# A two-layer encoder trunk on one core: the order of a few weight splits, a norm's tiles, and where one layer's modulation sums stand

## The chip, the cores and the metric

The kernel runs on one core of a Trainium2 chip. The metric is the device time of one launch in microseconds (us): 2183.36 is the median of three runs of the kernel before. PE (TensorE) does the matrix products, ACT (ScalarE) and DVE (VectorE) the work on rows, POOL (GpSimd) a few small copies, SP (SyncE) starts the transfers. A matrix product writes into PSUM, which has eight banks here.

## What is computed

One sequence of 256 tokens with 2048 features passes two layers. Every layer has an attention part and an MLP, each behind a root-mean-square norm that is modulated by a vector `c`:

```python
for l in range(DEPTH):                                  # 2 layers
    mod = cond @ w_ada[l] + b_ada[l]                    # cond = silu(c); 2048 -> 6 * 2048
    sh_a, sc_a, g_a, sh_m, sc_m, g_m = split(mod, 6)
    h = rmsnorm(x) * (1.0 + sc_a) + sh_a
    proj = h @ w_in[l]
    out_a = diff_attention(...)                         # half of the heads
    q = rmsnorm(cq, q_norm_g[l]) @ w_uq[l]              # latent attention: the other half
    kv = rmsnorm(ckv, kv_norm_g[l]) @ w_ukv[l]          # k_nope and the values v_m
    out_b = mla_attention(...)
    x = x + g_a * (concat(out_a, out_b) @ w_o[l])
    h = rmsnorm(x) * (1.0 + sc_m) + sh_m
    y = square(relu(h @ w_mlp_in[l])) @ w_mlp_out[l]    # 2048 -> 8192 -> 2048
    x = x + g_m * y
return rmsnorm(x, final_norm_g)
```

## The kernel before

The residual `x` stays on the chip with features along the partitions: 16 blocks of 128 features by 256 tokens. All weights come from memory as float32, mostly in 1 MB tiles.

**Split weights.** `weights` (L142) loads a tile `raw` through SP's queue, ACT copies each half of it into a rounded `hi` (L151), and DVE subtracts to get the rest, `lo` (L154). Activations are split in the same way. A product is then three matmuls: hi by hi, hi by lo, lo by hi (`mac`, L192 to L194). There are four buffers for `hi`, four for `lo` and five for `raw`. `wides` (L203) does the MLP's first product for two weight tiles in a bank each.

**Modulation.** A row block of `w_ada` is one more 1 MB tile, `ada`, in the same five `raw` buffers. `ada_load` (L297) starts its transfer, `ada_sums` (L303) reduces it on DVE in one instruction (L310). `weights` counts a `rate` for each tile that it loads: each time that the count reaches one, one modulation tile is loaded and later summed. Each stretch of the program has its own rate. `most` limits how many loaded tiles are summed.

**Order.** Outside the blocks under `manual_schedule`, a scheduler orders the instructions of an engine by the dependences; `follow(a, b)` is an added dependence, without a wait on the chip if both are on one engine. Inside those blocks PE's order is that of the code.

**The four places of the change.**
- *Layer 0, latent values.* `up_v` (L795) loads `w_uv`. Its two `hi` copies follow `self.copied`, the last `copy` (L282) that the code had made: here the copy `aT` of a transposed attention matrix. The products with `w_uv` are L263 to L265.
- *Layer 0, end of the attention part.* The output product adds into `x` in pairs of feature blocks (`update`, L1119). For the last pair, `pair` (L219) puts both products in the two halves of one bank.
- *Layer 0, norm ahead of the MLP.* `rstd` (L554): ACT squares the last pair of blocks one by one (`sqa`, L542); PE sums every square over the features with a constant matrix of which one column is used (`sums`, L569); ACT takes the root of two columns (L577), DVE the reciprocal (L578); PE spreads the result over the partitions by transposes (L584), ACT copies that out of PSUM (`rstd`, L588). Then `modulated` (L655) makes the input `h` of the MLP two blocks at a time: `ht` on DVE (L663), `hi` on ACT (L666), `lo` on DVE (L667). `norm_then_by_k` (L696) feeds them into six banks `pk`, 12 of the MLP's 64 hidden blocks, with two 768-column weight tiles for each pair of blocks. The squared ReLU of these six banks (`relu2`, L1136: Relu L1139, Square L1143, split L185 and L186) comes in `mlp` (L938) behind the first pair of `wides`, whose own halves are joined by `joined` (L1125).
- *Layer 1, norm ahead of the MLP.* `ahead_rest` (L628) works on the sums of the norm beside products `pa` that don't need them yet, at a modulation rate of 0.6 (`RATE_K`). The argument `loads` keeps the rate as it was found until that step of the loop; here it is left at 0.

Of the kernel before, what the change touches and what calls it, by code (L numbers as in the profile page):

```python
# [105 lines left out]
class Trunk:  # L106
# [35 lines left out]
    def weights(self, src, width=2048, after=None):  # L142
# [4 lines left out]
        for i in range(2):  # L147
# [3 lines left out]
            ins = nc.scalar.activation(hi, v, AF.Copy)  # L151
            if after is not None:
                self.follow(ins, after)
            ins = nc.vector.tensor_tensor(lo, v, hi.bitcast(F32), ALU.subtract)  # L154
            if self.hold is not None:
                self.follow(ins, self.hold)
# [46 lines left out]
    def wides(self, srcs, xs):  # L203
# [5 lines left out]
        ws = [self.weights(src, nk * P) for src in srcs]  # L209
# [9 lines left out]
    def pair(self, srcs, xs):  # L219
        ps = self.bank("ps")  # L220
        for j, src in enumerate(srcs):
            self.tile_cols(ps[:, j], src, xs)
        return ps

# [4 lines left out]
    def by_k(self, banks, srcs, xs, k0, nk, n=4, whole=None):  # L229
# [3 lines left out]
        for b, src in enumerate(srcs):  # L233
# [5 lines left out]
            else:  # L239
                w = self.weights(src, width)  # L240
# [295 lines left out]
    def sumsq(self, acc, val, alone=False, scale=1.0):  # L536

        nc = self.nc
        if alone:
            for i in range(2):  # L540
                t = self.tp.tile([P, T], F32, tag="t", name=self.name("sqa"))
                nc.scalar.activation(t, val[:, i], AF.Square)  # L542
# [11 lines left out]
    def rstd(self, acc, n):  # L554

        return self.spread(*self.total(acc, n))
# [9 lines left out]
    def sums(self, ps, a, n, first, last):  # L566

        for t in range(2):
            self.nc.tensor.matmul(  # L569
                ps[:, 0, t : t + 1], a[:, t * P : (t + 1) * P], self.mean[n][:, :1],  # L570
# [3 lines left out]
    def root(self, ps):  # L574
        nc = self.nc
        r = self.s("root")
        nc.scalar.activation(r, ps[:, 0, :2], AF.Sqrt, bias=self.eps)  # L577
        nc.vector.reciprocal(r, r)  # L578
        return ps, r
# [116 lines left out]
    def norm_then_by_k(self, l, acc, sh, sc, src, n, nwhole, fill=(), early=()):  # L696


        r = self.rstd(acc, D) if l or sh else acc
        banks = self.open_banks(2 * n)  # L700
        h = []
        for p in range(8):
# [9 lines left out]
            h += self.modulated(r, k, self.mod[l, sh], self.mod[l, sc], whole, self.lo if p - 1 in early else None)  # L712
# [8 lines left out]
            for b in range(2):  # L721
                self.by_k(banks[b * n :], [src[l, p, b]], h, k, NK, 2 * n, whole)
# [13 lines left out]
    def layer(self, l, acc, st):  # L736
# [173 lines left out]
        with self.tc.manual_schedule(engines={mybir.EngineType.PE}) if l else nullcontext():  # L910
            for m in range(4, NK, 2):
# [3 lines left out]
                if l == 0 and m == NK - 2:  # L915
                    self.update(m, self.pair(srcs, o), g)
# [21 lines left out]
    def mlp(self, l, h, first, g):  # L938
# [4 lines left out]
        nxt = None if l == DEPTH - 1 else self.ahead(l + 1, 0, 1, io["w_a1"][0])  # L943
        for fb in range(NFB):
# [446 lines left out]
```

## Time and profile before

| | |
|---|---|
| three runs, us | 2185.09, 2180.95, 2183.36 |
| median, us | 2183.36 |
| profiled execution, us | 2182.21 |
| its span, us | 2180.4 |
| granted clock of PE, mean over the span | 0.998 of full speed |

The profile shows one execution, taken by the hardware. Its times are us from the start of the span. A row of the timeline holds the start, the duration of a run of like instructions, the engine and line, the output and input by the program's names, the count, and in brackets the idle time of the engine just before with the instruction that ended it. PE's instructions overlap, so their durations add up to more than the time between their starts. A row of the windows holds the stretch and its length, then for PE, PEld (weight loads), DVE, ACT and POOL the busy time and the count, then the granted clock (1.00 is full speed), the busy share of the transfer engines and GB/s.

### The profile page before, as it was taken

The page shows a single profiled execution, that of the slowest core. Times are in us where ns is not written, and L with a number is a line of the kernel's source. Part 1 is how long each engine was busy: PE and PEld are TensorE (multiplying, and loading weights), DVE is VectorE, ACT ScalarE, POOL GpSimd, SP SyncE. Part 2 cuts the span into 40 slices and gives each one's busy share as a digit, 9 for nine tenths or more (in the row PEclk, how much of TensorE's full clock was granted, in tenths as well). Part 3 has the DMA queues.
Part 4 walks back from the last instruction along what each step waited for, and adds up shares of the span by engine and source line. Part 5 has one row for each costly group of instructions (what it writes and reads, how often), then busy time and mean ns, then how long its engine had stood idle before and what let it go on. Part 6 is the DMA issues. An engine that isn't in the chain of part 4 may idle for free.

```text
span 2180.4 us, 30393 instructions
## 1 busy us (share of the span) xinstructions
PE 2157.0 (99%) x12016; PEld 1888.5 (87%) x12016; DVE 1606.6 (74%) x2160; ACT 1153.0 (53%) x1739; POOL 23.3 (1%) x43
## 2 busy tenths in 40 slices
PE   8999999999999999999999999999999999999998
PEld 7899898988888888888898888999888888888886
DVE  8999888887778778778798876798544545555566
ACT  6565664454455355355456565547446535534544
POOL 0000000000000000000001000000000000000000
PEclk9999999999999999999999999999999999999999
DMA  9987888799879888888777666686555555555552
GB/s 400 424 331 275 333 314 310 270 345 344 326 301 343 331 302 341 309 312 330 287 251 270 253 239 226 247 303 240 193 193 193 193 193 188 187 195 189 189 196 95
DMA packets 85538, 586.41 MB, mean 269 GB/s; under 512 B 9489, under 2 KB 9489, under 8 KB 19345
## 3 DMA queue, kind: packets, MB, share of 16 engines
q1 hardware_dynamic: 85106, 583.84, 72.7%
q8 instruction: 94, 1.54, 0.3%
q10 hardware_dynamic: 288, 0.62, 0.1%
q14 instruction: 50, 0.41, 0.1%
HBM read 582.33 MB, written 2.10 MB: 268 GB/s over the span
## 4 chain that ended last, share of the span: by engine, by line
PE 94%; DVE 3%; DMA 2%; ACT 1%; issue 0%; DVEq 0%; ACTq 0%
PE ps L213 25%; PE ps L216 13%; PE py L1092 11%; PE py L1090 11%; PE py L1094 11%; PE pk L249 3%; PE pk L194 2%; PE pk L193 2%; PE pk L192 2%; PE pv L263 1%; PE pv L264 1%; PE pv L265 1%; DVE ada L310 1%; PE pa L194 1%; PE pa L192 1%; PE pa L193 1%
## 5 line engine op out<-in xcount | busy, mean ns | idle before, releaser
L154 DVE TENSOR_TENSOR lo<-raw,hi 128x1024 fp32r<-128x1024 f32 (+1 forms) x720 | 849.8, 1196 | 475.0 <-ACT hi L151 305.9
L151 ACT ACTIVATE hi<-raw 128x1024 fp32r<-128x1024 f32 (+1 forms) x720 | 736.9, 1035 | 649.9 <-PE py L1094 361.5
L213 PE MATMUL ps<-h,hi 128*128 128x512 f32 x2016 | 471.0, 391 | 0.9 <-ACT hi L151 0.9
L213 PEld LDWEIGHTS ps<-h,hi 128*128 128x128 f32 x2016 | 375.0, 188 | 76.9 <-ACT hi L151 1.3
L310 DVE SCALAR_TENSOR_TENSOR ada<-ada,cond 128x2048 f32<-128x2048 f32 x191 | 435.4, 2286 | 2.8 <-ACT sqx L389 2.0
L1090 PE MATMUL py<-hi,hid 128*128 128x512 f32 x1024 | 326.6, 390 | 0.0
L1092 PE MATMUL py<-lo,hid 128*128 128x512 f32 x1024 | 326.1, 389 | 0.0
L1094 PE MATMUL py<-hi,hid 128*128 128x512 f32 x1024 | 325.9, 389 | 0.0
L216 PEld LDWEIGHTS ps<-h,lo 128*128 128x128 f32 x2016 | 250.2, 192 | 4.9
L216 PE MATMUL ps<-h,lo 128*128 128x256 f32 x2016 | 251.7, 283 | 0.0
L1092 PEld LDWEIGHTS py<-lo,hid 128*128 128x128 f32 x1024 | 192.3, 188 | 40.3 <-DVE lo L154 0.4
L1094 PEld LDWEIGHTS py<-hi,hid 128*128 128x128 f32 x1024 | 192.3, 188 | 40.0
L1090 PEld LDWEIGHTS py<-hi,hid 128*128 128x128 f32 x1024 | 191.3, 188 | 38.7
L1129 ACT ACTIVATE sum<-ps 128x256 f32<-128x256 f32 x110 | 42.1, 383 | 128.2 <-PE ps L216 127.9
L192 PE MATMUL pk<-h,hi 128*128 128x256 f32 x304 | 86.0, 289 | 2.3 <-ACT h L666 1.5
L194 PE MATMUL pk<-h,lo 128*128 128x256 f32 x304 | 85.7, 286 | 1.0 <-DVE lo L154 1.0
L193 PE MATMUL pk<-h,hi 128*128 128x256 f32 x304 | 86.1, 285 | 0.1
L186 DVE TENSOR_TENSOR hid<-relu,hid 128x256 fp32r<-128x256 f32 x128 | 48.3, 422 | 45.8 <-ACT hid L185 45.8
L249 PE MATMUL pk<-hf,w 128*128 128x256 f32 x288 | 63.2, 380 | 0.0
L249 PEld LDWEIGHTS pk<-hf,w 128*128 128x128 f32 x288 | 54.5, 190 | 7.8 <-ACT hf L671 0.5
L192 PEld LDWEIGHTS pk<-h,hi 128*128 128x128 f32 x304 | 58.5, 195 | 3.0 <-ACT h L666 1.8
L1139 ACT ACTIVATE relu<-sum 128x512 f32<-128x512 f32 x55 | 34.6, 630 | 48.0 <-DVE sum L1131 47.9
(271 smaller groups left out, 2583.5 us busy)
## 6 DMA issues: line engine op xcount, KB each, us to landing
raw<-in_w_m SPq DMA_DIRECT2D x238, 1024.0 KB, 4.9
ada<-in_w_ada SPq DMA_DIRECT2D x191, 1024.0 KB, 5.0
raw<-in_w_ob SPq DMA_DIRECT2D x24, 1024.0 KB, 4.9
raw<-in_w_dv SPq DMA_DIRECT2D x16, 1024.0 KB, 4.9
raw<-in_w_q SPq DMA_DIRECT2D x16, 1024.0 KB, 4.8
raw<-in_w_n SPq DMA_DIRECT2D x16, 768.0 KB, 5.9
w<-in_w_a SPq DMA_DIRECT2D x24, 384.0 KB, 13.1
raw<-in_w_a SPq DMA_DIRECT2D x12, 768.0 KB, 5.8
```

The source lines that it names most:

```text
L151: ins = nc.scalar.activation(hi, v, AF.Copy)
L154: ins = nc.vector.tensor_tensor(lo, v, hi.bitcast(F32), ALU.subtract)
L192: mm(ps, hi, x[0], start=first, stop=False, skip_group_check=shared)
L193: mm(ps, hi, x[1], start=False, stop=False, skip_group_check=shared)
L194: mm(ps, lo, x[0], start=False, stop=last, skip_group_check=shared)
L213: mm(ps.rearrange("p a b -> p (a b)"), part(w, 0, k), both, start=k == 0, stop=False)
L216: mm(ps[:, 0], part(w, 1, k), x, start=False, stop=k == nk - 1)
L249: self.nc.tensor.matmul(ps, w[i][:, j * P : j * P + P], whole[i], start=first, stop=last, skip_group_check=True)
L310: ins = nc.vector.scalar_tensor_tensor(w, w, 1.0, self.cond, ALU.mult, ALU.mult, accum_out=acc[:, i : i + 1])
L1090: mm(o, xh[:, tok], hi[:, part[j]], start=start, stop=False)
L1092: mm(o, xh[:, tok], lo[:, part[j]], start=False, stop=False)
L1094: mm(o, xl[:, tok], hi[:, part[j]], start=False, stop=stop)
```

## The change

- `up_v` in layer 0: the `hi` copies of `w_uv` follow `spun`, the last `qr` copy of `up_r`, instead of the `aT` copy. On ACT the order of these five goes from `qr, qr, aT, hi, hi` to `qr, qr, hi, hi, aT`.
- The last pair of the output product in layer 0: two banks, each added into `x` as it is done; `pair` is gone.
- `sums` uses all 128 columns of the constant, so that every one of 128 columns holds the sum; `root` reads one column of each half. `rstd` also returns the spread in PSUM, and the first `modulated` of the norm reads it there (`near`). The copy L588 is still made for the others.
- In that norm's first step, the second weight tile's second `hi` follows the last `sqa`, and its second `lo` follows the reciprocal.
- The first Relu of the six banks follows the norm's last `hi`, the next ones the `hi` copies of the first `wides`.
- Layer 0's first `wides` in the MLP: its `joined` and `relu2` come after the second `wides` (`held`).
- Layer 1's norm: rate 0 until step 5 of `ahead_rest`.

The diff, with unchanged lines and the removal of `pair` cut:

```diff
     def weights(self, src, width=2048, after=None, first=0):
...
-            ins = nc.scalar.activation(hi, v, AF.Copy)
-            if after is not None:
+            ins = self.high = nc.scalar.activation(hi, v, AF.Copy)
+            if after is not None and i >= first:
                 self.follow(ins, after)
             ins = nc.vector.tensor_tensor(lo, v, hi.bitcast(F32), ALU.subtract)
-            if self.hold is not None:
+            if self.hold is not None and i >= first:
                 self.follow(ins, self.hold)
...
     # wides
+        ws, self.highs = [], []
+        for src in srcs:
+            ws.append(self.weights(src, nk * P))
+            self.highs.append(self.high)
...
     # by_k
-                w = self.weights(src, width)
+                w = self.weights(src, width, after, int(after is not None))
...
     def rstd(self, acc, n):
-        return self.spread(*self.total(acc, n))
+        ps, r = self.total(acc, n)
+        return self.spread(ps, r), ps[:, 1]
...
     # sums
-                ps[:, 0, t : t + 1], a[:, t * P : (t + 1) * P], self.mean[n][:, :1],
+                ps[:, 0, t * P : (t + 1) * P], a[:, t * P : (t + 1) * P], self.mean[n],
...
     # norm_then_by_k
-        r = self.rstd(acc, D) if l or sh else acc
+        r, near = self.rstd(acc, D) if sh else (acc, acc)
...
+            of = r if p else near
+            h += self.modulated(of, k, self.mod[l, sh], self.mod[l, sc], whole, self.lo if p - 1 in early else None)
...
             for b in range(2):
-                self.by_k(banks[b * n :], [src[l, p, b]], h, k, NK, 2 * n, whole)
+                later = self.squared if sh and p == 0 and b else None
+                if later:
+                    self.hold = self.inverse
+                self.by_k(banks[b * n :], [src[l, p, b]], h, k, NK, 2 * n, whole, later)
...
         def up_r():
             raw = [self.copy(ps, "qr", ms) for ps in self.small(io["w_uq"][l, 2], cq, 4)]
+            self.spun = self.copied
...
         def up_v():
-            w = self.weights(io["w_uv"][l], after=None if l else self.copied)
+            w = self.weights(io["w_uv"][l], after=None if l else self.spun)
...
                 if l == 0 and m == NK - 2:
-                    self.update(m, self.pair(srcs, o), g)
+                    pss = [self.bank("ps")[:, 0] for _ in srcs]
+                    for ps, src in zip(pss, srcs):
+                        self.tile_cols(ps, src, o)
+                    self.update(m, pss, g)
...
-            self.rate = RATE_K
+            self.rate = 0.0 if st else RATE_K
             if st:
-                h = self.ahead_rest(st, 0, acc, 2)
+                h = self.ahead_rest(st, 0, acc, 2, 5)
...
-                first = NNORM, lambda: [self.relu2(b) for b in banks]
-                first = NNORM, lambda: [self.relu2(b) for b in banks]
+                high = self.high
+                first = NNORM, lambda: [
+                    self.relu2(b, after=a) for b, a in zip(banks, [high, *self.highs, *self.highs[1:] * 3])
+                ]
...
     # mlp
-                hid += self.relu2(self.joined(pss, self.t("sum")))
+                    if l == 0:
+                        held = [pss]
+                        continue
+                for ps in held + [pss]:
+                    hid += self.relu2(self.joined(ps, self.t("sum")))
+                held = []
...
     # relu2
-            self.nc.scalar.activation(r, ps, AF.Relu)
+            ins = self.nc.scalar.activation(r, ps, AF.Relu)
+            if after is not None:
+                self.follow(ins, after)
```

What the change does to the engines' orders is shown at three places. The rows are in program order; numbers behind a name tell buffers of one name apart, and `x2` stands for two like instructions in a row. First DVE before, at the norm ahead of layer 0's MLP (`lo` L154 of the first weight tiles, `x` the last update, `root` the reciprocal, `ht` the first modulated blocks):

```order
L154 TENSOR_TENSOR lo_3892<-raw_3889,hi_3891 128x768
L154 TENSOR_TENSOR lo_3896<-raw_3889,hi_3895 128x768
L154 TENSOR_TENSOR lo_3938<-raw_3935,hi_3937 128x768
L1123 SCALAR_TENSOR_TENSOR x<-ps_3730,mod_83,x 128x256 x2
L154 TENSOR_TENSOR lo_3942<-raw_3935,hi_3941 128x768
L578 RECIPROCAL root_3867<-root_3867 128x2
L663 SCALAR_TENSOR_TENSOR ht_3880<-x,mod_87,rstd_3872 128x256 x2
```

and DVE there after the change:

```order
L1138 SCALAR_TENSOR_TENSOR x<-ps_3730,mod_83,x 128x256
L154 TENSOR_TENSOR lo_3893<-raw_3890,hi_3892 128x768
L154 TENSOR_TENSOR lo_3897<-raw_3890,hi_3896 128x768
L154 TENSOR_TENSOR lo_3939<-raw_3936,hi_3938 128x768
L1138 SCALAR_TENSOR_TENSOR x<-ps_3731,mod_83,x 128x256
L576 RECIPROCAL root_3868<-root_3868 128x2
L154 TENSOR_TENSOR lo_3943<-raw_3936,hi_3942 128x768
L661 SCALAR_TENSOR_TENSOR ht_3881<-x,mod_87,pn_3859 128x256 x2
```

The first of the two `x` updates has moved ahead of three `lo`, the fourth `lo` from before the reciprocal to behind it, and `ht` reads `pn`, the spread in PSUM.

Second, ACT at the end of that norm, before (`pk` are the six banks, `hi` of 768 columns the norm's last weight tile, `hi` of 1024 columns the first tile of the first `wides`; the second tile's two `hi` come eleven rows further on):

```order
L1139 ACTIVATE relu_4820<-pk_3874 128x512
L1143 ACTIVATE relu_4820<-relu_4820 128x512
L151 ACTIVATE hi_4681<-raw_4679 128x768
L151 ACTIVATE hi_4685<-raw_4679 128x768
L185 ACTIVATE hid_4823<-relu_4820 128x256
L185 ACTIVATE hid_4824<-relu_4820 128x256
L1139 ACTIVATE relu_4829<-pk_3875 128x512
L1139 ACTIVATE relu_4838<-pk_3876 128x512
L151 ACTIVATE hi_4732<-raw_4730 128x1024
L151 ACTIVATE hi_4736<-raw_4730 128x1024
```

and after the change:

```order
L151 ACTIVATE hi_4682<-raw_4680 128x768
L151 ACTIVATE hi_4686<-raw_4680 128x768
L1154 ACTIVATE relu_4821<-pk_3875 128x512
L1160 ACTIVATE relu_4821<-relu_4821 128x512
L185 ACTIVATE hid_4824<-relu_4821 128x256
L185 ACTIVATE hid_4825<-relu_4821 128x256
L151 ACTIVATE hi_4733<-raw_4731 128x1024
L151 ACTIVATE hi_4737<-raw_4731 128x1024
L1154 ACTIVATE relu_4830<-pk_3876 128x512
L1160 ACTIVATE relu_4830<-relu_4830 128x512
```

Each pair of `hi` now stands ahead of the Relu and Square that were in front of it; the second tile's two `hi` follow two rows further on.

Third, DVE in layer 1's norm, before (`ada` the modulation sum, `al` the low part of the products' input, `lo` the weights of `pa`):

```order
L154 TENSOR_TENSOR lo_13528<-raw_13525,hi_13527 128x768
L154 TENSOR_TENSOR lo_13532<-raw_13525,hi_13531 128x768
L310 SCALAR_TENSOR_TENSOR ada_13471,macc_102<-ada_13471,cond 128x2048
L614 SCALAR_TENSOR_TENSOR al_13510<-x,mod_99,ah_13509 128x256 x2
L578 RECIPROCAL root_13522<-root_13522 128x2
L154 TENSOR_TENSOR lo_13596<-raw_13593,hi_13595 128x768
```

and after the change:

```order
L154 TENSOR_TENSOR lo_13527<-raw_13524,hi_13526 128x768
L154 TENSOR_TENSOR lo_13531<-raw_13524,hi_13530 128x768
L154 TENSOR_TENSOR lo_13594<-raw_13591,hi_13593 128x768
L612 SCALAR_TENSOR_TENSOR al_13509<-x,mod_99,ah_13508 128x256 x2
L154 TENSOR_TENSOR lo_13598<-raw_13591,hi_13597 128x768
L576 RECIPROCAL root_13521<-root_13521 128x2
```

The sum between the weight splits is gone. It and a second one of the same norm, which stood just ahead of `lo_13726`, come some 30 rows later, in the MLP, and their two loads move back by six places on SP.

More of the change, by code (lines that the diff above doesn't have):

```diff
@@ L139, in bank, with weights @@
         return self.pp.tile([P, 2, T], F32, tag="b", name=self.name(name))
-    def weights(self, src, width=2048, after=None):
+    def weights(self, src, width=2048, after=None, first=0):
         nc = self.nc
@@ L217, in wides, with by_k @@
         return pss
[L219 to L223, printed above, removed]
     def open_banks(self, n):
         return [self.bank("pk") for _ in range(n)]
-    def by_k(self, banks, srcs, xs, k0, nk, n=4, whole=None):
+    def by_k(self, banks, srcs, xs, k0, nk, n=4, whole=None, after=None):
         kpb = srcs[0].shape[-1] // (n * P)
```

11 lines of the change are left out of this document (5 added, 6 removed).

## The prediction

> **What bounds the kernel now.** I read the page first, for the shares of the engines and of the chain that ended last, then the windows:
>
> ```profile
> PE 2157.0 (99%) x12016; PEld 1888.5 (87%) x12016; DVE 1606.6 (74%) x2160; ACT 1153.0 (53%) x1739; POOL 23.3 (1%) x43
> ...
> DVE  8999888887778778778798876798544545555566
> ...
> PE 94%; DVE 3%; DMA 2%; ACT 1%; issue 0%; DVEq 0%; ACTq 0%
> ```
>
> ```profile
> 585.00:1060.00 475.00, 475.00 (x2457) 408.77 (x2456) 375.70 (x431) 241.57 (x321) 6.55 (x6) 1.00 0.85 322
> 385.00:480.00 95.00, 89.71 (x704) 86.95 (x703) 80.68 (x113) 45.36 (x74) 0.00 (x0) 0.98 0.83 309
> ```
>
> PE is the bound: 99% busy, 94% of the chain, and between 585 and 1060 us without one gap. No PE work goes away, so the change can win only where PE stands still or runs at a lower clock. All its places together hold little of that: in layer 0's norm, 385 to 480 us, PE is busy for 89.71 of 95 us, and the granted clock is 0.98. A few microseconds of 2182 is the scale. The third step was PE's waits, and the timeline of PE around each. What a wait costs is seen in layer 1's norm:
>
> ```profile
> 1480.67 0.28 PE L192 MATMUL pa<-ah,hi 128*128 128x258 f32 x1
> 1480.79 0.28 PE L193 MATMUL pa<-al,hi 128*128 128x258 f32 x1
> 1482.20 0.39 PE L194 MATMUL pa<-ah,lo 128*128 128x258 f32 x1 [1.13 <-DVE lo L154]
> 1482.42 0.28 PE L192 MATMUL pa<-ah,hi 128*128 128x258 f32 x1
> ```
>
> Steady matmuls of this kind start 0.12 us apart (the first two rows). Then the starts are 1.41 and 0.22 apart: 1.29 and 0.10 too much, 1.39 in all, for a shown idle time of 1.13. So I add 0.26 to each wait that a row shows.
>
> **Layer 1's norm.** What the late `lo` waited for stands in DVE's timeline:
>
> ```profile
> 1478.12 2.28 DVE L310 SCALAR_TENSOR_TENSOR ada<-ada,cond 128x2048 f32<-128x2048 f32 x1
> ...
> 1481.19 0.95 DVE L154 TENSOR_TENSOR lo<-raw,hi 128x768 fp32r<-128x768 f32 x1
> ```
>
> The modulation sum ends at 1480.40, in front of the small steps of the norm and of this `lo`. With it gone, 2.28 us leave DVE's queue ahead of a wait of 1.4: all of it goes, and about 0.9 is left before the same `lo` is late again. **Gain 1.4.** The two sums come back 32 rows later in DVE's order, in the MLP, with their loads; from about 1525 us the page's DVE slices stand at 4 to 6 tenths, so 4.6 us more fit there. Cover gone would mean a late Relu of a bank, at most the same 2.28 less what slack is there.
>
> **Layer 0's value weights.** ACT's timeline, DVE's, and the PE wait:
>
> ```profile
> 211.54 0.60 ACT L282 ACTIVATE qr<-pss 128x512 f32<-128x512 f32 x1 [2.28 <-PE pss L194]
> 213.79 0.60 ACT L282 ACTIVATE aT<-pt 128x512 f32<-128x512 f32 x1 [1.65 <-PE pt L1218]
> 214.28 2.00 ACT L151 ACTIVATE hi<-raw 128x1024 fp32r<-128x1024 f32 x2
> ```
>
> ```profile
> 216.03 1.22 DVE L154 TENSOR_TENSOR lo<-raw,hi 128x1024 fp32r<-128x1024 f32 x1
> ```
>
> ```profile
> 215.39 0.73 PE L263 MATMUL pv<-hi,lath 128*128 128x512 f32 x2 [1.20 <-ACT hi L151]
> ```
>
> ACT stood idle for 1.65 us in front of `aT`, with the two `hi` queued behind it; PE then waited 1.20 for the first `hi`, 1.46 with the 0.26. Now the `hi` go into that idle stretch and PE's wait for them ends. But its next products need `lo`. The first `lo` starts at 216.03 with no idle time before it, so DVE had other work until then, and `hi` being earlier doesn't move it; it is ready at 217.25, while PE would want it 1.46 earlier than now. Part of the gain is eaten there, between nothing and all of it: 0 to 1.46. PE can take other products first (the order of PE puts a few score products ahead of those with `lo`), so I take the middle, **gain 0.7**. `aT` now queues behind 2.00 us of `hi`, and starts up to 1.7 us later than 213.79; PE's `pv` products stand in front of those that need it.
>
> **Layer 0's norm.** The chain runs through all engines:
>
> ```profile
> 395.54 0.95 PE L569 MATMUL pn<-mean,acc 128*128 128x1 f32 x8
> 396.87 1.05 PE L569 MATMUL pn<-mean,sqa 128*128 128x1 f32 x8 [0.38 <-ACT sqa L542]
> 398.47 0.43 PE L584 MATMUL pn<-ident,root 128*128 128x128 f32 x2 [0.55 <-DVE root L578]
> 400.44 1.65 PE L192 MATMUL pk<-h,hi 128*128 128x256 f32 x6 [1.53 <-ACT h L666]
> ```
>
> ```profile
> 396.42 0.71 ACT L542 ACTIVATE sqa<-x 128x256 f32<-128x256 f32 x2
> ...
> 398.94 0.38 ACT L588 ACTIVATE rstd<-pn 128x256 f32<-128x256 f32 x1 [0.72 <-PE pn L584]
> ```
>
> ```profile
> 395.74 0.88 DVE L1123 SCALAR_TENSOR_TENSOR x<-ps,mod,x 128x256 f32<-128x256 f32 x2
> 396.54 0.96 DVE L154 TENSOR_TENSOR lo<-raw,hi 128x768 fp32r<-128x768 f32 x1
> 398.25 0.17 DVE L578 RECIPROCAL root<-root 128x2 f32<-128x2 f32 x1 [0.75 <-ACT root L577]
> 399.36 1.28 DVE L663 SCALAR_TENSOR_TENSOR ht<-x,mod,rstd 128x256 f32<-128x256 f32 x3 [0.94 <-ACT rstd L588]
> ...
> 403.72 0.48 DVE L663 SCALAR_TENSOR_TENSOR ht<-x,mod,rstd 128x256 f32<-128x256 f32 x1
> 405.36 0.96 DVE L154 TENSOR_TENSOR lo<-raw,hi 128x768 fp32r<-128x768 f32 x1 [1.16 <-ACT hi L151]
> ```
>
> Both `x` updates waited for one bank; now the first is done early, and only one of 0.44 is left: the squares and the reciprocal come about 0.5 earlier, near 397.8. The copy `rstd`, 0.38 and its hand-over, leaves the way to the first `ht`: another 0.4, and `ht` could start near 398.4. But the `lo` of 0.96 that ran at 396.54, beside the squares, now stands behind the reciprocal: 397.9 to 398.9. So `ht` starts at 398.9, and the gain at the first `ht` is 399.36 less 398.9: 0.46. The first product of 400.44 moves by as much.
>
> Then comes the clock:
>
> ```profile
> 396.60:400.00 3.40, 1.48 (x10) 1.16 (x10) 1.71 (x5) 1.29 (x5) 0.00 (x0) 1.00 0.42 123
> 400.00:403.40 3.40, 2.96 (x14) 2.96 (x15) 3.40 (x10) 2.15 (x5) 0.00 (x0) 0.50 0.31 128
> 17.70:21.10 3.40, 1.53 (x8) 0.99 (x6) 3.27 (x3) 1.08 (x2) 0.00 (x0) 1.00 1.00 424
> 21.97 3.84 PE L337 MATMUL pf<-ccol,raw 128*128 128x128 f32 x32 [2.74 <-DMA raw<-in_w_adat]
> ```
>
> From 400.0 to 403.4 PE was granted half of its speed: 2.96 us of work that takes 1.48 at full speed. Ahead of it lies a stretch with 1.48 us of PE work by the records, in which no idle time exceeds the 1.53 of the row at 400.44. But 17.70 to 21.10 us, with 1.53 us of work, was followed by no drop: the 32 matmuls at 21.97 ran 0.12 apart. The two differ in their kind of work: in the one, eight of ten records are matmuls of one column. So I hold that these count for nearly nothing, and that 128 columns (the change) count. The Trainium skill, page "TensorE: Matmul & The Clock Gate", section "The HAM clock gate", says that the gate halves the rate after a free-running window of about 3.4 us in which the array was too idle, and offers as a rule of thumb to have no gaps of 3 us; the length of the half-rate stretch here, 3.4 us, agrees, the rule of thumb doesn't, with a longest gap of 1.53.
>
> If the clock stays up, PE wins up to 1.48 more, and the next bound is DVE: its `ht` of 403.72 comes 0.46 earlier, ends at 403.74, and the `lo` behind it, which waited 1.16 for a `hi` whose buffer the slow PE gave back late, follows at once: 403.74 instead of 405.36, 1.62 earlier. **Gain 1.6 with the clock up, 0.46 without**; between nothing and 0.46 + 1.48 = 1.94.
>
> The widened sums themselves I put at nothing. Eight of one column take 0.95 us, 0.12 each; 32 of 128 columns, at 21.97, take 3.84, 0.12 each. By the section "Back-to-back issue gap" of the same page of the Trainium skill, which prices a matmul by its columns, the 16 would be dearer by an estimated 0.05 each, 0.85 in all; the rows show no such difference.
>
> **End of that norm.** Two PE waits and what ACT did ahead of them:
>
> ```profile
> 467.66 0.60 ACT L1139 ACTIVATE relu<-pk 128x512 f32<-128x512 f32 x1 [2.85 <-PE pk L194]
> ...
> 468.83 1.56 ACT L151 ACTIVATE hi<-raw 128x768 fp32r<-128x768 f32 x2
> ...
> 478.02 2.00 ACT L151 ACTIVATE hi<-raw 128x1024 fp32r<-128x1024 f32 x2
> ```
>
> ```profile
> 469.70 0.39 PE L192 MATMUL pk<-h,hi 128*128 128x256 f32 x1 [0.65 <-ACT hi L151]
> 479.13 1.20 PE L213 MATMUL ps<-h,hi 128*128 128x512 f32 x4 [0.91 <-ACT hi L151]
> ```
>
> The norm's last `hi` waited behind a Relu and its Square, 468.83 less 467.66 = 1.17; PE waited 0.65 for it, 0.9 with the 0.26. With the `hi` in front that goes. The second tile's `hi` at 478.02 stood behind five Relus and their Squares; PE waited 0.91, 1.2 with the 0.26. Now only one bank's work is ahead of it. The first pair's join comes a pair later; what ACT then has to do ahead of the second pair's `hi` is the rest of the six banks, for which the first pair's 32 products of 512 and 32 of 256 columns give cover. **Gain 2.1**, the whole of both waits; nothing if the six banks' late Relus hold up the buffers `hid` or the second pair instead.
>
> **The sum.** 0.7 + 1.6 + 2.1 + 1.4 = 5.8. The profiled execution took 2182.21 (span 2180.4 and 1.8 around it): 2176.4. It lies 1.15 under the median of the three runs, 2183.36; I add half of that, as the next median can fall on either: **2177.0**. A measurement tells about 0.2% of this kernel from no change, 4.4 us: under 2179.0 is faster, above 2187.7 slower.
>
> **The rivals.**
> 1. *The clock drops all the same.* The one-column sums would then not be what let it fall, and the light stretch is, with 3 to 4 us between the output product and the first `pk`. For it: the stretch stays nearly as long, and its phase to the gate's window may shift. Against it: the row of 17.70 to 21.10. The norm then wins 0.46 instead of 1.6, 1.1 less: 2178.1. (By the rule of thumb of the Trainium skill's page "TensorE: Matmul & The Clock Gate", section "The HAM clock gate", no gap here was long enough to matter before, and none would be after: it has no reason for a difference, which is this case.) Chance 0.2.
> 2. *Given back.* The `lo` of the value weights is as late as it was, and in the norm the DVE chain gives back what the front of it wins: only 2.1 + 1.4 = 3.5 stay, 2178.7 and 0.6: 2179.3. For it: DVE is the next in line at both places, by the rows at 216.03 and 396.54. Chance 0.25.
> 3. *Slower: a weight transfer slips.* In layer 0's attention weights and modulation share five buffers, and the chain that ended last holds a wait for a whole transfer:
>
> ```profile
> 210.85 7.71 DMA raw<-in_w_uq
> ```
>
> If the moved `hi` copies give buffers back in another order, so that a weight's transfer comes behind one more transfer on SP's queue, PE waits for it; this one took 7.71. It decides once a landing is more than about 2 us later than now, an estimate of the slack from ACT's idle times of 2.28 and 1.65 in front of `qr` and `aT`. Two such misses, 15.4, give 2192.4. Against it: SP's order is the same up to layer 1. Chance 0.05.
> 4. *The change does nothing*, since other waits stood close behind each one: 2182.8. Chance 0.03.
>
> **Numbers.** The forecast has the remaining 0.47. The range: on the low side the value weights' 1.46 instead of 0.7 (0.76), the norm at 1.94 (0.34), no addition for the median (0.6), and about 1.0 for its scatter: 2174.3. On the high side rival 2 and the 1.7 by which the highest of the three runs lies above the median: 2181.0. Faster holds nearly all of the forecast, three quarters of rival 1 and a fifth of rival 2: 0.63. Slower, 0.06, is rival 3 and a little more. The rest, 0.31, is no difference that can be told.
>
> **What would show it.** Right: no `[.. <-ACT hi]` at the first `pv` product; the `lo` of the norm at about 403.7 less the shift so far, and the granted clock at 1.00 there; no wait at the norm's last `pk` and at the second tile of the first `wides`; no `<-DVE lo` in layer 1's `pa`. Wrong: a clock event of 0.50 near 400; a new `<-DVE lo` at `pv`, or `<-ACT aT` behind it; waits of PE for `hid` or for banks after 480; a new DMA wait before 390.

## The result, and the profile after

The changed kernel takes 2176.74 us, the median of seven runs (2175.09 to 2179.76), against 2183.49 for seven runs of the kernel before (2180.95 to 2185.09): ratio 0.9971, 95% interval 0.9959 to 0.9983. A second set of runs gave 2177.80 against 2182.72, 0.9974 (0.9963 to 0.9984). The gain was 6.75 us in the first set and 4.9 in the second. The forecast was 2177.0.

The profiled execution took 2177.76 us, with a span of 2176.0. That is only 4.4 less than before, because in this one execution the clock dropped at the very start, at 23.16 us, where the profile of before has no drop: the first product `pqr` of layer 0 starts at 213.29 us instead of 211.34. That drop is not a part of the change, as will be seen. First PE's waits after the change, all of them (times in total, count, longest):

```profile
PE pf L334 <- DMA raw<-in_w_adat: 3.9, 1, 3.9
PE pc L375 <- DMA c_row<-in_c: 2.8, 1, 2.8
PE pk L192 <- ACT h L664: 1.5, 1, 1.5
PE pn L582 <- DVE root L576: 0.6, 1, 0.6
PE psm L1283 <- DVE sm L1285: 0.5, 1, 0.5
PE pk L194 <- DVE lo L154: 0.5, 1, 0.5
PE pv L261 <- DVE lo L154: 0.5, 1, 0.5
PE pn L567 <- DVE mod L320: 0.4, 1, 0.4
PE pn L567 <- DVE acc L548: 0.3, 1, 0.3
```

Gone in this profile are the waits for `hi` at `pv`, `pk` and `ps`, for `lo` at layer 1's `pa`, and for `sqa`. One is new: `pv` now waits 0.5 for a `lo`. The wait for `h` at the first `pk` of the norm is as long as it was.

Layer 0's norm after the change, on PE, then ACT, then DVE:

```profile
396.60 1.05 PE L567 MATMUL pn<-mean,acc 128*128 128x128 f32 x8
397.49 1.06 PE L567 MATMUL pn<-mean,sqa 128*128 128x128 f32 x8
399.10 0.43 PE L582 MATMUL pn<-ident,root 128*128 128x128 f32 x2 [0.55 <-DVE root L576]
401.06 0.97 PE L192 MATMUL pk<-h,hi 128*128 128x256 f32 x6 [1.53 <-ACT h L664]
```

```profile
399.56 0.38 ACT L586 ACTIVATE rstd<-pn 128x256 f32<-128x256 f32 x1 [0.72 <-PE pn L582]
```

```profile
398.88 0.17 DVE L576 RECIPROCAL root<-root 128x2 f32<-128x2 f32 x1 [1.60 <-ACT root L575]
398.96 0.94 DVE L154 TENSOR_TENSOR lo<-raw,hi 128x768 fp32r<-128x768 f32 x1
399.98 0.87 DVE L661 SCALAR_TENSOR_TENSOR ht<-x,mod,pn 128x256 f32<-128x256 f32 x2
```

From the first sum to the first product of the norm it is 401.06 less 396.60, 4.46 us; before it was 400.44 less 395.54, 4.90. The second group of sums starts without a wait. But `ht` starts 0.04 us after the end of ACT's copy (399.56 and 0.38), although it reads PSUM and not the copy.

And the clock, in the same windows of 3.41 us in which it changed (the columns as before: PE's busy time and count first, the granted clock third from the end):

```profile
19.75:23.16 3.41, 0.72 (x6) 0.72 (x7) 3.28 (x5) 0.00 (x0) 0.00 (x0) 1.00 1.00 412
23.16:26.57 3.41, 3.41 (x18) 3.41 (x18) 3.07 (x8) 1.96 (x5) 0.00 (x0) 0.50 1.05 434
398.63:402.04 3.41, 1.41 (x10) 1.17 (x11) 3.08 (x8) 1.95 (x5) 0.00 (x0) 1.00 0.34 61
402.04:405.45 3.41, 3.41 (x18) 3.41 (x18) 2.77 (x8) 1.36 (x3) 0.00 (x0) 0.50 0.43 178
```

The norm's drop is still there, 2 us later in the program than before. It was forecast to go.

To find where time came from I compare the starts of named PE instructions in the traces; each column is the time between two of them, in us. *Values*: first `pqr` product of layer 0 to the first sum of its second norm. *Sums*: from there to the first `pk`. *Norm*: from the first sum to the first `wides` product. *First pair*: from there to the first `py` product. *Layer 1*: its first `pa` product to its first `wides` product. *Drop*: a half-rate window in layer 0's norm.

| kernel | values | sums | norm | first pair | layer 1 | drop |
|---|---|---|---|---|---|---|
| before | 184.20 | 4.90 | 78.86 | 23.43 | 37.53 | yes |
| changed | 183.31 | 4.46 | 76.31 | 22.23 | 35.77 | yes |
| changed, second profile | 183.31 | 4.47 | 77.52 | 22.22 | 35.78 | yes |

The rest behind the first `pqr`, 960 us from the first `py` to layer 1's first `pa` and 676 us from layer 1's first `wides` to the last product, agrees within 0.1 us.

### The profile page after: what moved, and what is told of

It reads as the page before. It is cut to its first block, busy times and chain, and to the rows that moved or that the text cites. A ratio compares the mean times of both kernels' runs of the same rounds, so it can differ in the third digit from the quotient of the medians.

```text
span 2176.0 us, 30393 instructions
## 1 busy us (share of the span) xinstructions
PE 2155.8 (99%) x12016; PEld 1889.2 (87%) x12016; DVE 1607.0 (74%) x2160; ACT 1154.5 (53%) x1739; POOL 22.4 (1%) x43
## 4 chain that ended last, share of the span: by engine, by line
PE 96%; DVE 2%; DMA 1%; ACT 1%; issue 0%; DVEq 0%; ACTq 0%
PE ps L216 25%; PE ps L219 13%; PE py L1107 11%; PE py L1105 11%; PE py L1109 11%; PE pk L246 3%; PE pk L194 2%; PE pk L193 2%; PE pk L192 2%; PE pv L261 2%; PE pv L262 2%; PE pv L260 1%; PE pa L194 1%; PE pa L193 1%; PE pa L192 1%; DVE ada L307 1%
## 5 line engine op out<-in xcount | busy, mean ns | idle before, releaser
L154 DVE TENSOR_TENSOR lo<-raw,hi 128x1024 fp32r<-128x1024 f32 (+1 forms) x720 | 848.4, 1194 | 466.0 <-ACT hi L151 293.8
```

## The experiments

All are edits of the changed kernel, timed against the kernel before on the same chip; ratios have their 95% intervals. The table has the same columns as above for each, and the text takes them in turn. Where a run was expected to differ by a microsecond, its ratio alone can't decide, as the intervals are 0.002 wide, 4 us; the stages of the traces can: the sums, the first pair and layer 1 repeat to 0.1 us where nothing is edited, the values to 0.7, the norm to about one.

| run | ratio | values | sums | norm | first pair | layer 1 | drop |
|---|---|---|---|---|---|---|---|
| undo_values | 0.9976 (0.9965–0.9987) | 184.43 | 4.46 | 76.75 | 22.23 | 35.78 | yes |
| undo_norm | 0.9974 (0.9964–0.9985) | 183.30 | 4.91 | 77.13 | 22.23 | 35.85 | yes |
| undo_relu | 0.9980 (0.9971–0.9990) | 183.97 | 4.46 | 78.36 | 23.47 | 35.78 | yes |
| undo_rate | 0.9985 (0.9975–0.9994) | 183.30 | 4.47 | 75.49 | 22.23 | 37.81 | no |
| narrow | 0.9974 (0.9963–0.9984) | 183.31 | 4.35 | 76.83 | 22.23 | 35.76 | yes |
| copy | 0.9972 (0.9963–0.9981) | 183.31 | 4.47 | 76.46 | 22.23 | 35.79 | no |
| near_apart | 0.9969 (0.9958–0.9979) | 183.29 | 4.21 | 74.66 | 22.23 | 35.78 | no |
| fill_norm | 0.9976 (0.9966–0.9987) | 183.69 | 6.10 | 76.52 | 22.23 | 35.76 | no |
| fill_both | 0.9970 (0.9958–0.9981) | 183.26 | 6.11 | 76.01 | 22.23 | 35.78 | no |
| fill_start | 0.9968 (0.9956–0.9981) | 183.48 | 4.47 | 76.57 | 22.22 | 35.78 | yes |
| best | 0.9966 (0.9952–0.9979) | 183.31 | 4.22 | 74.86 | 22.22 | 35.79 | no |

**The value weights' order undone.**

```diff
-            w = self.weights(io["w_uv"][l], after=None if l else self.spun)
+            w = self.weights(io["w_uv"][l], after=None if l else self.copied)
```

> The changed kernel, but the value weights' two hi copies of layer 0 follow the aT copy again. If the parts add (the theory of the prediction), PE waits for hi at the first pv product again, 1.2 us shown, the 0.5 us wait for lo that the changed kernel has there goes, and everything behind is 0.7 to 0.9 us later: ratio to the kernel before about 0.9974 where the changed kernel had 0.9971. If later waits absorb it (the rival that gains are given back), the wait is there but the output product's end is at the same place, and the later waits of PE for DVE shrink by as much.

PE's row at `pv` is that of before again:

```profile
PE pv L260 <- ACT hi L151: 1.2, 1, 1.2
```

The stage takes 184.43 us instead of 183.31, 1.1 more. The next stages are as in the changed kernel, so nothing there gives it back. The parts add here.

**The norm's parts undone**, all of them (the bank for two products, one-column sums, the copy's reader, the moved `hi` and `lo`):

```diff
-                    pss = [self.bank("ps")[:, 0] for _ in srcs]
-                    for ps, src in zip(pss, srcs):
-                        self.tile_cols(ps, src, o)
-                    self.update(m, pss, g)
+                    ps = self.bank("ps")
+                    for j, src in enumerate(srcs):
+                        self.tile_cols(ps[:, j], src, o)
+                    self.update(m, ps, g)
...
-            of = r if p else near
+            of = r
...
-                later = self.squared if sh and p == 0 and b else None
+                later = None
```

> The changed kernel, but layer 0's norm as before: last pair in one bank, one-column sums, the first ht behind ACT's copy, no moved hi and lo. If the parts add: PE's wait for sqa is back (0.4 us shown), from the first sum to the first pk product 4.9 us instead of 4.46, the clock drop as the phase has it, and 0.5 to 1.6 us lost in all: ratio 0.9973 to 0.9979. If it is given back, the end of the norm's products comes at the same distance from the first raw weight of the norm, and the ratio stays 0.9971.

The sums take 4.91 again, 0.44 more, and the wait for `sqa` is back:

```profile
PE pn L567 <- ACT sqa L539: 0.4, 1, 0.4
```

But the norm as a whole takes 77.13, between the 76.31 and 77.52 of the changed kernel's two profiles. What becomes of the 0.44 is seen near 424 us. Here is ACT there in the changed kernel's second profile and then in this run:

```profile
423.47 1.58 ACT L151 ACTIVATE hi<-raw 128x768 fp32r<-128x768 f32 x2 [5.08 <-DMA raw<-in_w_n]
```

```profile
422.66 1.58 ACT L151 ACTIVATE hi<-raw 128x768 fp32r<-128x768 f32 x2 [3.88 <-DMA raw<-in_w_n]
```

In both a weight's transfer ends last, and PE waits for this `hi` or its `lo` whatever it won before. Counted from the first sum (395.97 and 395.58 us), the `hi` starts at 27.50 us in the changed kernel and at 27.08 here: the weight came 0.42 later, and the 0.44 are gone. In the changed kernel's first profile (first sum at 396.60) PE passed the place without a wait. So of the 0.44 some or all is given back, as that transfer falls. The run's ratio, 0.9974, where the changed kernel has 0.9971 and 0.9974, fits this, but can't show a difference so small.

**The Relus in their old order.**

```diff
-                first = NNORM, lambda: [
-                    self.relu2(b, after=a) for b, a in zip(banks, [high, *self.highs, *self.highs[1:] * 3])
-                ]
+                first = NNORM, lambda: [self.relu2(b) for b in banks]
...
-                    if l == 0:
-                        held = [pss]
-                        continue
```

> The changed kernel, but the six banks' Relus and the join of the first pair of wides in their old order. If the parts add: the two waits of PE for hi are back, about 0.65 and 0.9 us, and 2.1 to 2.4 us are lost: ratio 0.9981. If it is given back, one of the two comes back, or none, and the time stays within 1 us.

Both waits are back, as two rows of PE's timeline show:

```profile
469.48 0.39 PE L192 MATMUL pk<-h,hi 128*128 128x256 f32 x1 [0.65 <-ACT hi L151]
...
478.90 3.48 PE L216 MATMUL ps<-h,hi 128*128 128x512 f32 x14 [0.93 <-ACT hi L151]
```

The first pair takes 23.47 instead of 22.23, 1.24 more, and the norm 78.36, 1.4 more than the mean of the changed kernel's two profiles, 76.92. Together 2.7, of which the second term has the norm's own scatter of a microsecond in it. (Its values stage is 0.7 longer by a wait of PE for `osq`, which no edit touches.)

**Layer 1's rate undone.**

```diff
-            self.rate = 0.0 if st else RATE_K
+            self.rate = RATE_K
             if st:
-                h = self.ahead_rest(st, 0, acc, 2, 5)
+                h = self.ahead_rest(st, 0, acc, 2)
```

> The changed kernel, but layer 1's norm with its modulation rate of 0.6 from the start. If the parts add: PE waits 1.1 us for a lo at about 1476 to 1478, and 1.4 to 1.8 us are lost, none of it given back by the end, as PE has no other wait behind it: ratio 0.9978. If another order of the same sums hides them, there is no such wait and the ratio is 0.9971.

PE waits for the `lo` again, and DVE's rows show the same modulation sum ahead of it:

```profile
1480.40 0.39 PE L194 MATMUL pa<-ah,lo 128*128 128x258 f32 x1 [1.24 <-DVE lo L154]
```

```profile
1476.32 2.29 DVE L307 SCALAR_TENSOR_TENSOR ada<-ada,cond 128x2048 f32<-128x2048 f32 x1
...
1479.40 0.95 DVE L154 TENSOR_TENSOR lo<-raw,hi 128x768 fp32r<-128x768 f32 x1
```

The stage takes 37.81 instead of 35.77: 2.0 lost, a little more than expected. Behind it the two programs run alike to the end.

**One-column sums alone.**

```diff
-                ps[:, 0, t * P : (t + 1) * P], a[:, t * P : (t + 1) * P], self.mean[n],
+                ps[:, 0, t : t + 1], a[:, t * P : (t + 1) * P], self.mean[n][:, :1],
```

> The changed kernel with one-column sums in place of 128 columns; all else as changed. Prediction's reason: a half-rate window in the norm in nearly all runs, mean clock 0.998 or less, 1.1 us more than the changed kernel. Rival: as often and as dear as in the changed kernel, some runs at 0.999, no difference in the median beyond 0.5 us. Price of the width itself: the eight records from the first sqa sum take 1.06 us with 128 columns; with one column 0.95 to 1.05 if the width is free.

The sums take 4.35 instead of 4.46: the width costs 0.11 us and wins nothing on this path. The clock dropped, but so it did in the two profiles with 128 columns and in three of the runs above and below. In the single runs, the highest mean clock with one column is 0.998 in 15 runs (this kernel and undo_norm), while 4 of 15 runs of the changed kernel show 0.999. That could hint that width helps now and then, but undo_values, with 128 columns, shows none in eight runs either; these runs don't settle it.

**Idle matmuls in the norm.** Eight matmuls on the constant matrix, two ahead of the transposes and six behind, into the bank `pn`:

```diff
+    def fill(self, out, n, after):
+        for _ in range(n):
+            ins = self.nc.tensor.matmul(out, self.mean[D], self.mean[D], start=True, stop=True, skip_group_check=True)
+            self.follow(ins, after)
+        return ins
...
+            self.fill(ps[:, 1, :P], 2, self.summing)
...
+            self.fill(ps[:, 0, :P], 6, turn)
```

> The changed kernel with eight idle matmuls of 128 columns more on PE in layer 0's norm, in the two gaps around the transposes (two ahead, six behind, results unused). If the clock is judged by PE's work in a window, no run drops there any more, and where the changed kernel drops in a run, this one saves 0.5 to 1.6 us; in the median 0.5 to 1.5 us faster than the changed kernel. If the drop has another cause, it stays, and the time is equal or, where the idle matmuls are in the way of the first pk product, up to 0.5 us slower.

The drop in the norm is gone; the clock stays at 1.00 through it, and the profile's only drop ahead of the end is at the start. But the sums take 6.10, 1.64 more. ACT's row and DVE's timeline say why:

```profile
401.00 0.38 ACT L598 ACTIVATE rstd<-pn 128x256 f32<-128x256 f32 x1 [2.36 <-PE pn L581]
```

```profile
398.76 0.94 DVE L154 TENSOR_TENSOR lo<-raw,hi 128x768 fp32r<-128x768 f32 x1
401.42 0.87 DVE L673 SCALAR_TENSOR_TENSOR ht<-x,mod,pn 128x256 f32<-128x256 f32 x2 [1.73 <-ACT rstd L598]
```

`ht` waits for ACT's copy, and the copy for the six idle matmuls (L581) in its bank, though these write other columns. What the clock won the wait took: 76.52 for the norm, and a median of 2177.72 us where the changed kernel has 2177.80 on the same chip; the 0.5 to 1.5 us that were expected did not come.

**Idle matmuls at the start too.** Eleven more in front of the first `pf` product, into its bank, here and in fill_start, which has these eleven alone:

```diff
         out = self.bank("pf")[:, 0, :P]
+        self.fill(out, 11, self.lastpn)
```

> As the one before, and eleven more idle matmuls at the start, where PE waits 2.7 to 3.9 us for the first modulation tile. If work in the window decides, the drop that the changed kernel's profile shows at 23.16 us is gone in all runs, all runs have a mean clock of 0.999, and the spread between runs, 4.7 us for the changed kernel, shrinks to 2 or less; the median 1 to 2 us below the changed kernel. If not, the clocks vary as before.

> The changed kernel with eleven idle matmuls on PE while it waits for the first modulation tile, nothing in the norm. If work in the window decides, no drop near 22 us in any run: 3.68 us from the first pf matmul to the first pk, where a drop makes it 5.2; the mean clock 0.998 or 0.999 in all runs, and the median 0.7 to 1.4 us below the changed kernel (2177.8 with seven runs of fifteen at two or more half-rate windows). If the drop at the start is absorbed by later waits for transfers, the median is the same.

The profile of fill_both has no half-rate window ahead of the end, and its six runs lie between 2175.85 and 2177.51, a spread of 1.7 instead of 4.7; the mean clock is 0.999 in three of them and 0.998 in three, not 0.999 in all. The three profiles with idle matmuls at the start (these two and the last run below) have no drop there; of the eleven without them, eight have one. From the first `pf` to the first `pk` it takes 3.68 us in both, as in the profile of before, where a drop makes it 5.2 to 6.4 in the runs that have one. The median is 2176.47 for both. For fill_both that is 1.3 below the changed kernel's 2177.80 on the same chip, a step that the intervals don't resolve. Some of the 1.5 is given back: from that first `pk` to layer 0's `pqr` it takes 186.29 with the idle matmuls and 185.54 after a drop.

**The copy's reader undone.**

```diff
-            of = r if p else near
+            of = r
```

> The changed kernel, but the norm's first ht reads ACT's copy of the spread again and not PSUM. By the prediction the copy of 0.38 us left the way of the first ht, and the lo held behind the reciprocal then filled most of that; so without it ht would start up to 0.1 us later than now and from the first sum to the first pk product 4.5 to 4.6 us. Rival, from the run with idle matmuls, where ht starts 0.04 us after the copy's end and not after PE's: ht waits for the copy in the changed kernel too, and it stays at 4.46.

4.47 and 4.46: reading PSUM directly wins nothing in this program. Both programs start `ht` when ACT's copy is done.

**Two banks for the spread**, with the moved `hi` and `lo` undone:

```diff
+        two = self.bank("pm")[:, 1]
+        for t in range(2):
+            self.nc.tensor.transpose(two[:, t * P : (t + 1) * P], r[:, t : t + 1].broadcast_to([P, P]), self.ident)
-        return self.spread(ps, r), ps[:, 1]
+        return self.spread(ps, r), two
...
-                later = self.squared if sh and p == 0 and b else None
+                later = None
```

> The changed kernel, but the spread is made twice, in two banks, the first for the first ht and the second for ACT's copy, and the second weight tile's hi and lo are no longer moved. If ht waits in the changed kernel because ACT and DVE read one bank in turn, it now starts right after PE's transposes: 0.4 us less from the first sum to the first pk product, about 4.1. If ht was held by the lo behind the reciprocal alone, the same 4.0 to 4.1. If it is held by something else, 4.4 to 4.5. At the end of the norm 0 to 0.4 of it is left: the waits for weights near 424 and 446 us take the rest if they are bound by the transfers.

The first product now waits 0.90 for `h` instead of 1.53, and DVE's `ht` waits for PE alone:

```profile
399.25 0.87 DVE L666 SCALAR_TENSOR_TENSOR ht<-x,mod,pm 128x256 f32<-128x256 f32 x2 [0.59 <-PE pm L556]
```

The sums take 4.21. That is 0.25 less, not 0.4, since with the `hi` in its old place the reciprocal comes 0.1 later. The run undoes two things at once. In the changed kernel the `lo` held behind the reciprocal ended at 399.90 us and ACT's copy at 399.94, so either would have held `ht` about as long. That the copy does hold it is seen in fill_norm, where the `lo` was long done.

The norm's clock stayed up in this profile. The norm's light window and the one behind it are

```profile
397.55:400.97 3.42, 1.88 (x14) 1.48 (x14) 2.42 (x7) 1.77 (x5) 0.00 (x0) 1.00 0.52 174
400.97:404.38 3.41, 3.41 (x31) 3.41 (x30) 3.41 (x9) 2.38 (x6) 0.00 (x0) 1.00 0.19 75
```

The first began 1.44 us behind the first sum, a place at which the changed kernel has its drop (see the next section). The earlier product and the two transposes more brought the window's work to 1.88 us.

**All of it.** The two banks, the moved `hi` and `lo` undone, and idle matmuls at the start (eleven) and in the norm (two and four, in a bank of their own):

```diff
+        two, idle = self.bank("pm")[:, 1], self.bank("pf")[:, 0, :P]
+        self.fill(idle, 2, self.summing)
+        for t in range(2):
+            turn = self.nc.tensor.transpose(two[:, t * P : (t + 1) * P], r[:, t : t + 1].broadcast_to([P, P]), self.ident)
+        out = self.spread(ps, r)
+        self.fill(idle, 4, turn)
+        return out, two
```

> The changed kernel with what the runs so far point to: the spread twice in two banks, the moved hi and lo of the norm undone, eleven idle matmuls in the wait at the start and six in the norm's gaps, these in a bank of their own. If a window of 3.41 us with less than about 1.5 to 1.8 us of PE work is what halves the clock, no run has a half-rate window before the end: 3.68 us from the first pf matmul to the first pk, 4.2 us from the first sum to the first pk product of the norm, 74.6 us or a little less from the first sum to the first wides; median 2174.5 to 2176, below the 2176.5 of the runs with idle matmuls and the 2177.8 of the changed kernel. If the waits for weights in the norm set its end, the norm takes 75 to 76 us and the median is 2176 to 2177.

No drop before the end, 4.22 for the sums, 74.86 for the norm, median 2175.70 of five runs (2173.84 to 2177.68). What the six idle matmuls of the norm do is not shown by this profile: its windows of 3.41 us begin with the first sum, and in `copy`, a norm without idle matmuls, two windows laid like that hold 2.41 and 2.32 us of PE work, so this execution would have had no drop there anyway. The median is the lowest of the changed kernel and its eleven variants. The interval of its ratio to before, 0.9966 (0.9952 to 0.9979), lies wholly below 1; the changed kernel's medians, 1.0 and 2.1 higher, are from other sets of runs and their intervals overlap with this one, so that it beats that kernel is likely, not shown.

## Why the prediction was right, and which step failed

The time and its sign were right, and three of the four terms had the right mechanism. The norm's term did not. Two of the prediction's own signs of being wrong came, too: the clock event near 400, and a new wait for `lo` at `pv`.

- **Value weights**, 0.7 forecast of 0 to 1.46: 0.9 between the profiles, 1.1 by the undone part. The `hi` wait went, and a wait for `lo` came, 0.5 shown, as the bound from the row at 216.03 had it: that `lo` starts 4.69 us behind the first `pqr` before and 4.68 after, so the earlier `hi` didn't move it.
- **End of the norm**, 2.1: the first pair wins 1.2, as forecast. The other wait, forecast at 0.9, went as well; undoing it cost 1.4 in a stage that varies by a microsecond.
- **Layer 1's rate**, 1.4: 1.76 between the profiles, 2.0 by the undone part. The price was read from the first late `lo` alone; the `pa` products had a second delay behind it, of 0.3.
- **The widened sums**, nothing: 0.11. The row decided better than the formula of the Trainium skill, page "TensorE: Matmul & The Clock Gate", section "Back-to-back issue gap", by which I had estimated 0.85.
- **The norm**, 1.6: this step failed. It said "I hold that these count for nearly nothing, and that 128 columns (the change) count", and so that the clock would stay up. But the drop stayed in five of the eight profiles with 128 columns and no idle matmuls in the norm. The rival *the clock drops all the same* is what happened; it priced the norm at 0.46, and the run with the norm undone shows that even this is partly given back near 424 us, where a transfer ends last. With all of the norm's parts undone, the norm takes 77.13 us, against a mean of 76.92 for the changed kernel's two profiles: 0.2 in place of 1.6, in a stage that varies by a microsecond.
- **The norm's first half**, 0.46: 0.44 was measured, and that it fits is in part luck. The prediction added 0.5 for the earlier squares and 0.4 for the copy that leaves the way, and took most of one back for the `lo` behind the reciprocal. Measured from the first sum, the reciprocal started at 2.71 us before and 2.28 after, which is the whole gain. The copy stayed in the way, and the `lo` ran beside it.

In place of that step the runs show two things. First, the time of the drop. In every trace all drops lie on one grid of 3.41 us: in the changed kernel's profile the clock went up at 12.92, down at 23.16 (3 steps later), up at 26.57 and down at 402.04 (110 steps later, 375.47 divided by 3.4133). The grid's start differs from run to run. A drop follows a window with little PE work in it, whatever the width of the sums. Three windows, from three kernels, each with the one behind it:

```profile
398.14:401.55 3.41, 1.73 (x12) 1.49 (x13) 3.32 (x8) 1.74 (x4) 0.00 (x0) 1.00 0.43 126
401.55:404.96 3.41, 3.41 (x19) 3.41 (x18) 2.58 (x8) 1.90 (x4) 0.00 (x0) 0.50 0.30 124
```

```profile
400.41:403.82 3.41, 1.82 (x13) 1.58 (x14) 3.32 (x9) 1.74 (x4) 0.00 (x0) 1.00 0.45 113
403.82:407.23 3.41, 3.41 (x31) 3.41 (x30) 3.41 (x8) 2.56 (x5) 0.00 (x0) 1.00 0.30 123
```

```profile
397.26:400.67 3.41, 3.06 (x27) 2.87 (x26) 1.02 (x2) 1.26 (x3) 0.00 (x0) 1.00 0.10 38
400.67:404.09 3.42, 1.89 (x16) 1.70 (x15) 2.67 (x7) 1.74 (x4) 0.00 (x0) 1.00 0.71 230
404.09:407.50 3.41, 3.41 (x30) 3.41 (x30) 3.41 (x9) 2.64 (x6) 0.00 (x0) 1.00 0.00 0
```

They are undo_relu, with 1.73 us of work and then half rate, undo_rate, with 1.82 and full rate, and fill_norm, with 1.89 and full rate. In the norm the border lies between 1.73 and 1.82 of 3.41 us, about half. At the start it lies lower: the prediction's window with 1.53 was followed by full rate, as were one with 1.59 (undo_relu) and one with 1.79 (narrow), and one with 1.39 (undo_values) by half rate:

```profile
18.17:21.58 3.41, 1.39 (x7) 0.88 (x5) 3.27 (x4) 1.08 (x2) 0.00 (x0) 1.00 1.01 423
21.58:25.00 3.42, 1.85 (x8) 1.85 (x9) 3.31 (x5) 0.00 (x0) 0.00 (x0) 0.50 1.03 414
```

Why the two places differ stays open. Another kind of work at the start is one possible reason. A small shift of the windows is another: taken 0.1 us earlier, undo_relu's window in the norm, with a drop behind it, holds 1.63 and its window at the start, with none, 1.59, so that one border near 1.6 isn't excluded. The Trainium skill, page "TensorE: Matmul & The Clock Gate", section "The HAM clock gate", gives 3413 ns and a window that runs freely; both agree with the grid here. That an idle window is needed does not: PE was at work for half of it.

So it is the phase, the place of the grid, that decides whether a given run has the drop, and the light stretch of the norm is about as light as before. Seven profiles have sums of 4.46 or 4.47 us and no idle matmuls in the norm. Where the window began 1.1 to 2.3 us behind the first sum the clock dropped (five of them); where it began 2.4 and 2.6 behind it (undo_rate and copy), it did not. With one-column sums it dropped at 1.0, 1.4 and 1.8. At the start a drop makes the stretch from `pf` to `pk` 1.5 us or more longer. What is left of a drop at the end of the norm is not settled: 76.3 to 77.5 us with one (changed, its second profile, undo_values, fill_start) and 75.5 and 76.5 without (undo_rate, copy) differ by 0.8 in the mean, in a stage that varies by a microsecond.

Second, the sum. By the table: 0.9 for the values, 1.76 for layer 1, 1.2 for the first pair and 1.9 for norm and last `hi` together (78.86 to 76.92), 5.8 in all, and the forecast was 5.8. The four undone parts cost 1.1, 0.2, 2.7 and 2.0, 6.0 in all, so nothing large is left over. That the sum fits is partly luck: the norm and the last `hi` gave 0.6 less than their 2.5, the values and layer 1 0.6 more than theirs.

The rival *given back* was right at one of its two places, the norm. At the other, the value weights, its condition held, as the `lo` was as late as before, but PE had other products to take first, and most of the gain stayed. A weight transfer that slips was not seen in layer 0's attention, where the third rival had it; the 0.6 us for a late weight near 424 us, in the changed kernel's second profile, is in the norm.

## What to carry to other kernels

When a wait is taken away from a PE-bound kernel, ask which stage sets its end: where the next product waits for a transfer (here at 424 us), what is won in front of it can be lost again, and where PE runs without a wait to the end (here layer 1), all of it stays, and the whole price is the difference between starts, not the idle time that one row shows. A short half-rate window belongs to the run as much as to the program; compare stages of traces with and without it before crediting a change. If it hurts, put PE work into the light stretch, in a bank that nobody is about to read.

## What was not expected of the hardware

- The clock changes only on a grid of 3.41 us that lies elsewhere in each run. In the norm a window in which PE worked for 1.73 us led to half rate, and one with 1.82 did not; at the start 1.39 did and 1.53 did not.
- Two readers of one PSUM bank were served in turn: with idle matmuls in the norm DVE stood idle for 1.73 us and started `ht` 0.04 us after ACT's copy of the same bank had ended (401.38 and 401.42); with a bank of its own, `ht` waited for PE alone. The Trainium skill, page "PSUM — Partial Sum Buffer", section "PSUM bank collisions raise a hardware error", says that the compiler adds a dependency between any two instructions of different engines that touch the same bank and 32-partition quadrant, two readers included; the rows here agree, and with that page read beside the change, the 0.4 us that the prediction credited to reading PSUM directly would have been left out.
